# SSD decays: running sums broadcast by DMA into SBUF, differences on VectorE

## The chip, the cores and the metric

The kernel runs on one core of a Trainium2 chip. The metric is the time of one execution on the device in microseconds, as the median of a few runs. A core has TensorE (PE: matmuls from SBUF into PSUM; its weight loads, PEld, overlap them), VectorE (DVE), ScalarE (ACT), GpSimd (POOL) and SyncE (SP), which here only issues DMAs. Each engine works through its own list of instructions in order and waits on semaphores for the others.

## The reference, cut to what matters

One decoder layer over 16 meta tokens and 1024 tokens, width 1024, in fp32: an RMSNorm and an input projection, then side by side a stick-breaking attention (8 heads), a Mamba-2 SSD mixer (16 heads of 64 channels, 2 groups, state 128) and a latent attention (MLA, 8 heads); an output projection; a SwiGLU MLP. The change touches the SSD mixer:

```python
dA = dt * a                                   # per token and head
Acs = cumsum(dA, axis=2)                      # running sum within a block of 128 tokens
seg = Acs[:, :, :, None] - Acs[:, :, None, :]
Ldec = exp(where(tri, seg, -inf))             # 128 x 128 decays per block and head
CB = einsum('bclgn,bcsgn->bclsg', Cc, Bc)
y_diag = einsum(..., CB[..., None] * Ldec, X)
decay = exp(Acs[:, :, -1:] - Acs)
states = einsum(..., Bc, X * decay[..., None])
chunk_decay = exp(Acs[:, :, -1])              # carry * chunk_decay + states, over the blocks
y_off = einsum(..., Cc, prev) * exp(Acs)[..., None]
```

## The kernel before, in words

All sequences are held feature-major (features over the partitions, tokens along the row), and the tokens fall into nine blocks: one of 16 meta tokens and eight of 128. Each large projection is done as three fp32r matmuls of a high and a low half (lines 144 to 146 for most, 908 to 910 for V). The program is written as units of work (projections, convolutions, attention rows, SSD chunks, latent projections). A scheduler lays them out: it runs through a simulated timeline and fixes the order of the instructions on each engine from priorities, dependences and the buffers that are free; while one unit waits, matmuls of others are put on TensorE ("fillers"). So an edit in one unit moves the instructions of its neighbours.

`running_sums` (line 461) is called early. One matmul with a triangle gives the running sums as `AT` (tokens over the partitions, 9 blocks x 16 heads). Each of three chunks of tokens is transposed to `acs` (16 heads over the partitions, tokens along the row), copied by ScalarE, and split on VectorE into three bf16 parts, rows 0, 32 and 64 of `A3` (lines 476 to 482).

`ssd_chunk(c)` (line 756) is called for the nine blocks, and in each for two groups g of eight heads. By name:
- `y` = xs times d_skip (GpSimd, line 765); `X` = transposed x times the step size (VectorE, 774).
- `R`: the running sum of four heads, equal over all 128 partitions. It is made by a matmul of the 0/1 matrix `sel` with `A3` for each head (line 794), into a pool of two PSUM tiles, `rps`.
- `cd`, `dec`: the block's decay and its decay to the block's end (796, 797, 811); `ea` = exp(R) (803); `L` = exp of minus the rectified difference AT - R (ScalarE: `Relu` per head, 806, then one `Exp`, 816).
- `Xd` = X times dec (GpSimd, 812); `cbm` = the product of the group's B and C under the triangle (818, 820); `L` times `cbm` (821).
- `yo`, `sps`, `yd`: the matmuls from the carried state (825), into the state (829), and within the block (841), in a pool of two PSUM tiles, `yps`. `ea` times `yo` (826), the state `S` times `cd` on GpSimd (833) and plus `sps` (836), `y` plus `ea` on GpSimd (846), `y` plus `yd` (847).
- `y` is stored by ScalarE's DMA queue; `xs` and `bc` (B and C) are loaded by SP's (761, 762).

Other names: `wlo` (133) is the low half of a weight, made on GpSimd; `grow` (518) sums squares of the SSD output on GpSimd; `Q` (614) is an eviction of the stick-breaking attention; `d_ps` is the PSUM tile of a projection; line 173 holds the transposes that spread a row of norms over the partitions; line 328 and `ptg` belong to the stick-breaking attention.

Of the kernel before, what the change touches and what calls it, by code (L numbers as in the profile page):

```python
# [11 lines left out]
F32 = mybir.dt.float32  # L12
F32R = mybir.dt.float32r
BF16 = mybir.dt.bfloat16
AF = mybir.ActivationFunctionType
ALU = mybir.AluOpType
AX = mybir.AxisListType
PSUM = bass.MemoryType.PSUM
# [5 lines left out]
META = 16  # L24
T = SEQ + META
# [34 lines left out]
def tile_hybrid_block(ctx: ExitStack, tc: tile.TileContext, a: dict):  # L60
    nc = tc.nc
    act, dve, pool, pe, sp = nc.scalar, nc.vector, nc.gpsimd, nc.tensor, nc.sync
# [10 lines left out]
    dram = ctx.enter_context(tc.tile_pool(name="dram", bufs=1, space=DRAM))  # L73
# [22 lines left out]
    s_qn = dram.tile([4, 128, SEQ], F32, name="s_qn")  # L96
    s_qr = dram.tile([2, 128, SEQ], F32, name="s_qr")
    s_v = dram.tile([9, 128, 512], F32, name="s_v")
    s_inv = dram.tile([MLA_HEADS, SEQ], F32, name="s_inv")


# [84 lines left out]
    keep = hn_stack.enter_context(tc.tile_pool(name="keep", bufs=1))  # L186
    AT = keep.tile([128, 9, 16], F32, name="AT")
    DT = keep.tile([128, 9, 16], F32, name="DT")
    A3 = keep.tile([80, T], BF16, name="A3")
    tri = keep.tile([128, 128], F32, name="tri")  # L190
    fl = hn_stack.enter_context(tc.tile_pool(name="fl", bufs=2))

# [268 lines left out]
    def running_sums(d1):  # L461
        NC = 9 * 16
        pt = tp.tile([128, 512], F32, tag="tp", name="acum")
        pe.matmul(pt[:, :NC], tri, d1, start=True, stop=True)
        dve.tensor_copy(AT.rearrange("p b h -> p (b h)"), pt[:, :NC])

        pool.memset(A3, 0.0)
        for i, (t0, n) in enumerate(CH_ALL):
            acs = fill_tile("craw" if i == 2 else "cacc", "acs")[:16]
            pt = tp.tile([128, 512], F32, tag="tp", name="acst")  # L470
            for b in range(3 * i, 3 * i + 3):
                b0, w = BLOCKS[b]
                pe.transpose(pt[:16, b0 - t0 : b0 - t0 + w], AT[:w, b, :], ident[:w, :w])
            c = slice(t0, t0 + n)
            act.copy(acs[:, :n], pt[:16, :n])
            dve.tensor_copy(A3[0:16, c], acs[:, :n])
            dve.tensor_tensor(acs[:, :n], acs[:, :n], A3[0:16, c], op=ALU.subtract)
            dve.tensor_copy(A3[32:48, c], acs[:, :n])
            a2 = fl.tile([16, 384], BF16, tag="csig", name="a2")
            dve.tensor_copy(a2[:, :n], acs[:, :n])  # L480
            dve.tensor_tensor(acs[:, :n], acs[:, :n], a2[:, :n], op=ALU.subtract)
            dve.tensor_copy(A3[64:80, c], acs[:, :n])

    def conv_unit(u):

# [163 lines left out]
    for i, (q0, qn) in enumerate(((0, 256), (256, 384), (640, 384))):  # L649
        c0, n = CH_ALL[i]  # L650
        if i < 2:
# [9 lines left out]
            r, row = stats[i]  # L661
# [80 lines left out]
    with ExitStack() as st:  # L742
        la = st.enter_context(tc.tile_pool(name="la", bufs=1, side="right", reuse_waits="tile"))
        p2_st = ExitStack()
        p2 = p2_st.enter_context(tc.tile_pool(name="p2", bufs=2, side="right", reuse_waits="tile"))
        rps = st.enter_context(tc.tile_pool(name="rps", bufs=2, space=PSUM, reuse_waits="tile"))
        yps = st.enter_context(tc.tile_pool(name="yps", bufs=2, space=PSUM, reuse_waits="tile"))
        seli = p2.tile([80, 16], F32, bufs=1, name="seli")
        sp.dma_start(seli, a["sel"])
        sel = p2.tile([80, 16, 128], BF16, bufs=1, name="sel")  # L750
        dve.tensor_copy(sel, seli.unsqueeze(2).to_broadcast([80, 16, 128]))
        dsk = p2.tile([128, 8], F32, bufs=1, name="dsk")
        sp.dma_start(dsk, a["d_skip"])
        S = [p2.tile([128, 512], F32, bufs=1, name=f"S{g}") for g in range(2)]
# [1 line left out]
        def ssd_chunk(c):  # L756
            n = META if c == 0 else 128
            t0 = 0 if c == 0 else META + 128 * (c - 1)
# [9 lines left out]
            for g in range(2):  # L768
                gs = slice(512 * g, 512 * (g + 1))
                hs = slice(8 * g, 8 * g + 8)  # L770
# [12 lines left out]
            for g in range(2):  # L783
                gs = slice(512 * g, 512 * (g + 1))
                hs = slice(8 * g, 8 * g + 8)
                cd = p2.tile([128, 8], F32, tag="cd", name="cd")
                dec = p2.tile([128, 8], F32, tag="dec", name="dec")
                L = p2.tile([128, 8, 128], F32, tag="L", name="L")
                ea = p2.tile([128, 4, 128], F32, tag="yt", bufs=1, name="ea")
                for q in range(2):  # L790
                    R = rps.tile([128, 4, 128], F32, tag="R", name="R")
                    qs = slice(4 * q, 4 * q + 4)
                    for h in range(4):
                        pe.matmul(R[:, h, :n], sel[:, 8 * g + 4 * q + h, :], A3[:, t0 : t0 + n], start=True, stop=True)
                    if c < 8:
                        act.activation(cd[:, qs], R[:, :, n - 1], AF.Exp)
                        dve.tensor_tensor(
                            dec[:n, qs], R[:n, :, n - 1], AT[:n, c, 8 * g + 4 * q : 8 * g + 4 * q + 4], op=ALU.subtract
                        )
                    if c > 0:  # L800
                        for e in range(2):
                            half = slice(64 * e, 64 * e + 64)
                            act.activation(ea[half, 2 * q : 2 * q + 2], R[half, e::2, :], AF.Exp)
                        for h in range(4):
                            hh = 4 * q + h
                            act.activation(
                                L[:, hh, :], R[:, h, :], AF.Relu, scale=-1.0,
                                bias=AT[:, c, 8 * g + hh : 8 * g + hh + 1],
                            )
                if c < 8:  # L810
                    act.activation(dec[:n], dec[:n], AF.Exp)
                    pool.tensor_tensor(
                        heads(Xd[:n, gs]), heads(X[:n, gs]), dec[:n].unsqueeze(2).to_broadcast([n, 8, 64]), op=ALU.mult
                    )
                if c > 0:
                    act.activation(L, L, AF.Exp, scale=-1.0)
                    pcb = tp.tile([128, 512], F32, tag="tp", name="cbp")
                    pe.matmul(pcb[:, :128], bc[:, g, :], bc[:, 2 + g, :], start=True, stop=True)
                    cbm = p2.tile([128, 128], F32, tag="cbm", name="cbm")
                    dve.tensor_tensor(cbm, pcb[:, :128], tri, op=ALU.mult)  # L820
                    dve.tensor_tensor(L, L, cbm.unsqueeze(1).to_broadcast([128, 8, 128]), op=ALU.mult)
                    yo = yps.tile([128, 512], F32, tag="y", name="yo")
                    for j in range(4):
                        ts = slice(128 * j, 128 * (j + 1))
                        pe.matmul(yo[:, ts], S[g][:, ts], bc[:, 2 + g, :], start=True, stop=True)
                    dve.tensor_tensor(ea, ea, yo.rearrange("p (j t) -> p j t", j=4), op=ALU.mult)
                if c < 8:
                    sps = yps.tile([128, 512], F32, tag="y", name="sps")
                    pe.matmul(sps, btok[:n, g * 128 : (g + 1) * 128], Xd[:n, gs], start=True, stop=True)
                    if c == 0:  # L830
                        dve.tensor_copy(S[g], sps)
                    else:
                        pool.tensor_tensor(
                            heads(S[g]), heads(S[g]), cd.unsqueeze(2).to_broadcast([128, 8, 64]), op=ALU.mult
                        )
                        dve.tensor_tensor(S[g], S[g], sps, op=ALU.add)
                if c > 0:
                    yd = yps.tile([128, 512], F32, tag="y", name="yd")
                    for h in range(8):
                        hh = 8 * g + h  # L840
                        pe.matmul(
                            yd[64 * (h % 2) : 64 * (h % 2) + 64, 128 * (h // 2) : 128 * (h // 2 + 1)],
                            X[:, hh * 64 : (hh + 1) * 64], L[:, h, :], start=True, stop=True,
                        )
                    yg = y[:, 4 * g : 4 * g + 4]
                    pool.tensor_tensor(yg, yg, ea, op=ALU.add)
                    dve.tensor_tensor(yg, yg, yd.rearrange("p (j t) -> p j t", j=4), op=ALU.add)
# [55 lines left out]
        for b, (t0, w) in enumerate(BLOCKS):  # L903
# [7 lines left out]
            t = row_tile("vtok")  # L911
# [18 lines left out]
        for c0, n in CH_SHORT:  # L930
            c = slice(c0, c0 + n)
# [767 lines left out]
def _layout(x, meta_tokens, mix_norm_g, w_in, conv_w, conv_b, dt_bias, a_log, d_skip, ssm_norm_g,  # L1699
# [16 lines left out]
    inv = (np.float32(10000.0) ** (-np.arange(0, 32, 2, dtype=np.float32) / np.float32(32))).astype(np.float32)  # L1716
    ang = (pos[:, None] * inv[None, :]).astype(np.float32)
    cos, sin = np.cos(ang).T.astype(np.float32), np.sin(ang).T.astype(np.float32)
    sel = np.zeros((80, 16), np.float32)
    for r in (0, 32, 64):  # L1720
        sel[r : r + 16] = np.eye(16)
    return {
        "xT": xn.T.reshape(KT, 128, T),
        "gmix": _cols(mix_norm_g[0]),
# [25 lines left out]
        "k_tab": np.concatenate([cos, cos, -sin, sin], axis=0),  # L1750
        "q_cos": np.tile(cos[:, META:], (8, 1)),
        "q_sin": np.tile(sin[:, META:], (8, 1)),
        "sel": sel,
    }


# [18 lines left out]
```

## Time and profile before

| | us |
|---|---|
| median of 3 runs | 1745.81 (1743.37 to 1752.36) |
| the profiled execution | 1744.0, its span 1742.3 |
| mean granted TensorE clock | 0.989 of full speed |
| busy: PE / DVE / ACT / POOL | 1688.7 (97%) / 1140.2 (65%) / 846.0 (49%) / 717.3 (41%) |
| running sums: instructions of `running_sums` on VectorE | 121.5 to 134.0 from the span's start |
| SSD stage | about 470 to 613 |

Times in the profile are microseconds from the span's start unless they are marked ns. A line of a group names the code line, engine, operation, output and input tile with their shapes, the count, the busy time and the mean ns of one, then the idle time of the engine ahead of it and what ended it. A line of the timeline has the start, the duration, the engine and line, and in brackets how long the engine had been idle and which instruction released it. The profile's time excludes what lies around the span; the runs' times include it (1744.0 against 1742.3).

### The profile page before, as it was taken

To read this page: it belongs to the slowest core of one execution; us is meant where nothing else is said; L and a number is where in the kernel's file an instruction comes from. 1 tells how busy PE (TensorE), PEld (TensorE's weight loads), DVE (VectorE), ACT (ScalarE), POOL (GpSimd) and SP (SyncE) were. 2 spreads that over 40 slices of the span, in tenths; PEclk is the share of its full clock that TensorE was granted. 3 is DMA by queue.
4 is the path that set the end of the run, shared out by engine and by line. 5 is a ranking of instruction groups with operands and counts; after the bars stand their busy time and mean duration, and the time that the engine had idled before them with its cause. 6 is when DMAs were issued, how large, how long until landed. Compare 5 with 4: busy or idle time off the path is not lost.

```text
span 1742.3 us, 26429 instructions
## 1 busy us (share of the span) xinstructions
PE 1688.7 (97%) x9673; PEld 1479.6 (85%) x9673; DVE 1140.2 (65%) x1773; ACT 846.0 (49%) x1811; POOL 717.3 (41%) x514
## 2 busy tenths in 40 slices
PE   8889999999999999999999999999999999999998
PEld 7879989999987888998888878788888888878887
DVE  7777676678455644556576556966666656688644
ACT  6555565656477727776455425432223222343333
POOL 3233335344567537553331445635555555200012
PEclk9999999999999999999999999999999999999999
DMA  4321232122534465348222452232322233999602
GB/s 164 72 67 62 69 89 80 59 69 78 154 115 121 149 219 167 107 130 282 68 78 65 103 180 73 70 99 92 114 91 97 96 104 106 328 398 358 235 1 98
DMA packets 145639, 222.35 MB, mean 128 GB/s; under 512 B 24722, under 2 KB 84148, under 8 KB 145508
## 3 DMA queue, kind: packets, MB, share of 16 engines
q1 hardware_dynamic: 126112, 205.09, 36.6%
q10 hardware_dynamic: 19396, 15.56, 2.9%
q8 instruction: 76, 1.25, 0.3%
q14 instruction: 55, 0.45, 0.1%
HBM read 157.56 MB, written 63.04 MB: 127 GB/s over the span
## 4 chain that ended last, share of the span: by engine, by line
PE 80%; DVE 6%; DMA 6%; ACT 3%; issue 2%; POOL 2%; SPq 0%; ACTq 0%; DVEq 0%; POOLq 0%
PE d_ps L144 9%; PE d_ps L146 9%; PE d_ps L145 9%; PE b_ps L1283 8%; PE b_ps L1282 8%; PE b_ps L1281 8%; PE b_ps L1566 2%; PE b_ps L1567 2%; PE b_ps L1565 2%; PE ptg L326 2%; PE ptg L328 1%; PE pv L305 1%; PE pv L304 1%; DMA raw<-s_osbl 1%; PE sc_ps L991 1%
## 5 line engine op out<-in xcount | busy, mean ns | idle before, releaser
L144 PE MATMUL d_ps<-hnh,whi 128*128 128x384 f32 (+6 forms) x744 | 247.4, 333 | 7.8 <-DVE KS L607 5.4
L146 PE MATMUL d_ps<-hnl,whi 128*128 128x384 f32 (+6 forms) x744 | 248.4, 334 | 0.0
L145 PE MATMUL d_ps<-hnh,wlo 128*128 128x384 f32 (+6 forms) x744 | 246.7, 332 | 0.1
L133 POOL TENSOR_TENSOR wlo<-wraw,whi 128x1024 fp32r<-128x1024 f32 (+1 forms) x57 | 136.8, 2401 | 218.2 <-ACT whi L131 194.1
L144 PEld LDWEIGHTS d_ps<-hnh,whi 128*128 128x128 f32 (+1 forms) x744 | 141.0, 190 | 12.7 <-issue 6.0
L146 PEld LDWEIGHTS d_ps<-hnl,whi 128*128 128x128 f32 (+1 forms) x744 | 140.8, 189 | 3.1 <-issue 0.7
L145 PEld LDWEIGHTS d_ps<-hnh,wlo 128*128 128x128 f32 (+1 forms) x744 | 140.9, 189 | 2.8 <-POOL wlo L133 0.4
L1282 PE MATMUL b_ps<-T,wl 128*128 128x512 f32 x352 | 139.6, 397 | 1.3 <-POOL wl L1113 1.3
L1283 PE MATMUL b_ps<-T,wh 128*128 128x512 f32 x352 | 139.2, 397 | 1.3 <-DVE T L1113 1.3
L1281 PE MATMUL b_ps<-T,wh 128*128 128x512 f32 x352 | 139.3, 397 | 0.0
L312 DVE TENSOR_TENSOR pl<-ptg,ph 128x512 fp32r<-128x512 f32 (+1 forms) x160 | 99.8, 628 | 55.3 <-ACT ph L311 54.1
L1112 ACT CAST op<-raw 128x1024 fp32r<-128x1024 f32 x69 | 71.2, 1050 | 111.3 <-PE d_ps L1567 55.1
L311 ACT CAST ph<-ptg 128x512 fp32r<-128x512 f32 (+1 forms) x160 | 85.6, 542 | 52.3 <-PE ptg L328 32.8
L1113 DVE TENSOR_TENSOR op<-raw,op 128x1024 fp32r<-128x1024 f32 x69 | 84.9, 1240 | 39.5 <-ACT op L1112 39.4
L696 DVE TENSOR_TENSOR_SCAN cm<-cm,sb_mask 128x144 f32<-128x144 f32 (+3 forms) x64 | 97.1, 1523 | 7.4 <-ACT cm L694 6.8
L1113 POOL TENSOR_TENSOR wlo<-raw,whi 128x1024 fp32r<-128x1024 f32 x18 | 45.4, 2521 | 110.3 <-ACT whi L1112 110.3
L1113 POOL TENSOR_TENSOR wl<-raw,wh 128x512 fp32r<-128x512 f32 x46 | 74.9, 1635 | 30.5 <-ACT wh L1112 30.3
L1112 ACT CAST wh<-raw 128x512 fp32r<-128x512 f32 x88 | 53.2, 616 | 69.5 <-PE b_ps L1283 69.4
L131 ACT CAST whi<-wraw 128x1024 fp32r<-128x1024 f32 (+1 forms) x57 | 58.9, 1033 | 55.4 <-PE d_ps L146 30.6
L1119 POOL TENSOR_TENSOR tt<-tt 128x512 f32<-128x512 f32 (+1 forms) x8 | 8.1, 1015 | 188.4 <-ACT tt L1637 188.2
L1282 PEld LDWEIGHTS b_ps<-T,wl 128*128 128x128 f32 x352 | 66.8, 190 | 17.4 <-POOL wl L1113 1.6
L1116 DVE TENSOR_TENSOR raw<-raw 128x512 f32<-128x512 f32 x58 | 53.2, 925 | 43.3 <-DMA raw<-in_w_gate_dram 38.4
(440 smaller groups left out, 5120.0 us busy)
## 6 DMA issues: line engine op xcount, KB each, us to landing
raw<-in_w_down_dram SPq DMA_DIRECT2D x99, 256.0 KB, 5.3
s_hops<-gs SPq DMA_DIRECT2D x63, 256.0 KB, 2.0
raw<-s_hops SPq DMA_DIRECT2D x63, 256.0 KB, 5.4
raw<-in_w_gate_dram SPq DMA_DIRECT2D x22, 512.0 KB, 3.6
raw<-in_w_up_dram SPq DMA_DIRECT2D x22, 512.0 KB, 4.2
wraw<-in_w_o_dram SPq DMA_DIRECT2D x16, 512.0 KB, 3.8
wraw<-in_w_xbc_dram SPq DMA_DIRECT2D x12, 512.0 KB, 4.2
s_xs<-csig SPq DMA_DIRECT2D x24, 192.0 KB, 2.6
```

The source lines that it names most:

```text
L133: pool.tensor_tensor(lo[:, :cols], raw[:, :cols], f32(hi[:, :cols]), op=ALU.subtract)
L144: pe.matmul(ps[:m, :n], wh, mh, start=(kt == 0), stop=False)
L145: pe.matmul(ps[:m, :n], wl, mh, start=False, stop=False)
L146: pe.matmul(ps[:m, :n], wh, ml, start=False, stop=(kt == nkt - 1))
L311: act.copy(ph[:, :n], pt[:, :n])
L312: dve.tensor_tensor(pl[:, :n], pt[:, :n], f32(ph[:, :n]), op=ALU.subtract)
L696: dve.tensor_tensor_scan(rev, rev, sb_mask[:, T - n_all :][:, ::-1], 1.0, ALU.mult, ALU.max)
L1112: act.copy(hi, value)
L1113: eng.tensor_tensor(lo, value, f32(hi), op=ALU.subtract)
L1281: pe.matmul(banks[j], hi[:, ks], UH[u][k], start=start and k == 0, stop=False, skip_group_check=skip)
L1282: pe.matmul(banks[j], lo[:, ks], UH[u][k], start=False, stop=False, skip_group_check=skip)
L1283: pe.matmul(banks[j], hi[:, ks], UL[u][k], start=False, stop=stop and k == 3, skip_group_check=skip)
```

## The change

The running sums are no longer split into bf16 parts. Each `acs` goes to a scratch array in DRAM, `s_sum` (9 blocks x 16 heads x 128 tokens), by SP's DMA queue. `ssd_chunk` then loads one tile `R` of 8 heads x 128 tokens per group from there, the same row into all 128 partitions, into SBUF with four buffers. The `sel` input, `A3`, the R matmuls and the PSUM pool `rps` are gone, and `yps` has four buffers instead of two. `cd`, `dec` and `ea` are computed for eight heads at once. `L` is made by VectorE: per head one `tensor_scalar` takes R minus the head's column of `AT`, and the smaller of that and 0; ScalarE's `Exp` then has scale 1 in place of -1. In the code after, most lines of this part carry other numbers: R's load is 782, `dec` 785, `ea` 789, the new operation 791, `Xd` 796, `L` exp 800, `L` times `cbm` 805, `yo` 809, `sps` 813, `S` 820, `yd` 825, `y` 830 and 831.

```diff
     s_v = dram.tile([9, 128, 512], F32, name="s_v")
+    s_sum = dram.tile([9, 16, 128], F32, name="s_sum")
...
     DT = keep.tile([128, 9, 16], F32, name="DT")
-    A3 = keep.tile([80, T], BF16, name="A3")
...
 
-        pool.memset(A3, 0.0)
         for i, (t0, n) in enumerate(CH_ALL):
             acs = fill_tile("craw" if i == 2 else "cacc", "acs")[:16]
             pt = tp.tile([128, 512], F32, tag="tp", name="acst")
             for b in range(3 * i, 3 * i + 3):
                 b0, w = BLOCKS[b]
                 pe.transpose(pt[:16, b0 - t0 : b0 - t0 + w], AT[:w, b, :], ident[:w, :w])
-            c = slice(t0, t0 + n)
             act.copy(acs[:, :n], pt[:16, :n])
-            dve.tensor_copy(A3[0:16, c], acs[:, :n])
-            dve.tensor_tensor(acs[:, :n], acs[:, :n], A3[0:16, c], op=ALU.subtract)
-            dve.tensor_copy(A3[32:48, c], acs[:, :n])
-            a2 = fl.tile([16, 384], BF16, tag="csig", name="a2")
-            dve.tensor_copy(a2[:, :n], acs[:, :n])
-            dve.tensor_tensor(acs[:, :n], acs[:, :n], a2[:, :n], op=ALU.subtract)
-            dve.tensor_copy(A3[64:80, c], acs[:, :n])
+            if i == 0:
+                sp.dma_start(s_sum[0, :, :META], acs[:, :META])
+            nb = min(3, n // 128)
+            src = acs[:, n - 128 * nb : n].rearrange("h (b t) -> h b t", b=nb)
+            sp.dma_start(s_sum[3 * i + 3 - nb : 3 * i + 3].rearrange("b h t -> h b t"), src)
...
         p2 = p2_st.enter_context(tc.tile_pool(name="p2", bufs=2, side="right", reuse_waits="tile"))
-        rps = st.enter_context(tc.tile_pool(name="rps", bufs=2, space=PSUM, reuse_waits="tile"))
-        yps = st.enter_context(tc.tile_pool(name="yps", bufs=2, space=PSUM, reuse_waits="tile"))
-        seli = p2.tile([80, 16], F32, bufs=1, name="seli")
-        sp.dma_start(seli, a["sel"])
-        sel = p2.tile([80, 16, 128], BF16, bufs=1, name="sel")
-        dve.tensor_copy(sel, seli.unsqueeze(2).to_broadcast([80, 16, 128]))
+        yps = st.enter_context(tc.tile_pool(name="yps", bufs=4, space=PSUM, reuse_waits="tile"))
...
                 ea = p2.tile([128, 4, 128], F32, tag="yt", bufs=1, name="ea")
-                for q in range(2):
-                    R = rps.tile([128, 4, 128], F32, tag="R", name="R")
-                    qs = slice(4 * q, 4 * q + 4)
-                    for h in range(4):
-                        pe.matmul(R[:, h, :n], sel[:, 8 * g + 4 * q + h, :], A3[:, t0 : t0 + n], start=True, stop=True)
-                    if c < 8:
-                        act.activation(cd[:, qs], R[:, :, n - 1], AF.Exp)
-                        dve.tensor_tensor(
-                            dec[:n, qs], R[:n, :, n - 1], AT[:n, c, 8 * g + 4 * q : 8 * g + 4 * q + 4], op=ALU.subtract
+                R = p2.tile([128, 8, 128], F32, tag="R", bufs=4, name="R")
+                sp.dma_start(R[:, :, :n], s_sum[c, hs, :n].partition_broadcast(128))
+                if c < 8:
+                    act.activation(cd, R[:, :, n - 1], AF.Exp)
+                    dve.tensor_tensor(dec[:n], R[:n, :, n - 1], AT[:n, c, hs], op=ALU.subtract)
+                if c > 0:
+                    for e in range(2):
+                        half = slice(64 * e, 64 * e + 64)
+                        act.activation(ea[half], R[half, e::2, :], AF.Exp)
+                    for h in range(8):
+                        dve.tensor_scalar(
+                            L[:, h, :], R[:, h, :], AT[:, c, 8 * g + h : 8 * g + h + 1], 0.0, op0=ALU.subtract, op1=ALU.min
                         )
-                    if c > 0:
-                        for e in range(2):
-                            half = slice(64 * e, 64 * e + 64)
-                            act.activation(ea[half, 2 * q : 2 * q + 2], R[half, e::2, :], AF.Exp)
-                        for h in range(4):
-                            hh = 4 * q + h
-                            act.activation(
-                                L[:, hh, :], R[:, h, :], AF.Relu, scale=-1.0,
-                                bias=AT[:, c, 8 * g + hh : 8 * g + hh + 1],
-                            )
                 if c < 8:
                     act.activation(dec[:n], dec[:n], AF.Exp)
                     pool.tensor_tensor(
                         heads(Xd[:n, gs]), heads(X[:n, gs]), dec[:n].unsqueeze(2).to_broadcast([n, 8, 64]), op=ALU.mult
                     )
                 if c > 0:
-                    act.activation(L, L, AF.Exp, scale=-1.0)
+                    act.activation(L, L, AF.Exp)
```

The scheduler lays the work out anew up to the end of the SSD stage; from the latent units after it TensorE's order is the same. Three places follow. The first is VectorE at the running sums; `Q` is an eviction of the stick-breaking attention. Before:

```order
L614 TENSOR_TENSOR Q<-d_ps,Q 64x512
L481 TENSOR_TENSOR acs<-acs,a_1085 16x272
L478 CAST A_119<-acs 16x384
L480 CAST a_1098<-acs 16x384
L482 CAST A_119<-acs 16x272
L614 TENSOR_TENSOR Q<-d_ps,Q 64x512
```

After:

```order
L465 COPY AT<-acum 128x144
L610 TENSOR_TENSOR Q<-d_ps,Q 64x512 x4
L319 TENSOR_TENSOR pm<-ptm,pm 16x256
L495 SCALAR_TENSOR_TENSOR cacc<-d_ps,cw,cacc 128x269
L495 SCALAR_TENSOR_TENSOR cacc<-d_ps,cw,cacc 128x270
```

The Q evictions stood between the casts and subtractions of the split; now they follow one another.

The second is VectorE in the middle of the SSD stage. Before:

```order
L820 TENSOR_TENSOR cbm<-cbp,tri 128x128
L847 TENSOR_TENSOR y<-y,yd 128x512
L826 TENSOR_TENSOR ea<-ea,yo 128x512
L821 TENSOR_TENSOR L<-L,cbm 128x1024
L797 TENSOR_TENSOR dec<-R,AT 128x4 x2
L820 TENSOR_TENSOR cbm<-cbp,tri 128x128
L836 TENSOR_TENSOR S_5436<-S_5436,sps 128x512
L847 TENSOR_TENSOR y<-y,yd 128x512
L774 TENSOR_TENSOR X<-xtp,DT 128x512
L826 TENSOR_TENSOR ea<-ea,yo 128x512
L821 TENSOR_TENSOR L<-L,cbm 128x1024
```

After:

```order
L831 TENSOR_TENSOR y<-y,yd 128x512
L791 TENSOR_SCALAR L<-R,AT 128x128 x8
L810 TENSOR_TENSOR ea<-ea,yo 128x512
L820 TENSOR_TENSOR S_5411<-S_5411,sps 128x512
L791 TENSOR_SCALAR L<-R,AT 128x128 x7
L765 TENSOR_TENSOR X<-xtp,DT 128x512
L791 TENSOR_SCALAR L<-R,AT 128x128
L785 TENSOR_TENSOR dec<-R,AT 128x8
L831 TENSOR_TENSOR y<-y,yd 128x512
L810 TENSOR_TENSOR ea<-ea,yo 128x512
```

The new operations of a group stand together, ahead of evictions (`ea`, `S`, `X`) for which TensorE and GpSimd wait.

The third is TensorE at the end of the SSD stage; `d_ps<-lhi` are the latent projections, `d_ps<-whi` those of V. Before:

```order
L144 MATMUL d_ps<-lhi,whi 128x384
L145 MATMUL d_ps<-lhi,wlo 128x384
L146 MATMUL d_ps<-llo,whi 128x384
L173 MATMUL d_ps<-identr,rc 128x128 x4
L841 MATMUL yd<-L,X 64x128 x8
L173 MATMUL d_ps<-identr,rc 128x128 x4
L144 MATMUL d_ps<-lhi,whi 128x512
L145 MATMUL d_ps<-lhi,wlo 128x512
```

After:

```order
L892 MATMUL d_ps<-whi,lhi 128x512
L893 MATMUL d_ps<-whi,llo 128x512
L825 MATMUL yd<-L,X 64x128 x8
L894 MATMUL d_ps<-wlo,lhi 128x512
L892 MATMUL d_ps<-whi,lhi 128x512
L893 MATMUL d_ps<-whi,llo 128x512
L894 MATMUL d_ps<-wlo,lhi 128x512
```

Behind the last `yd` now stand 19 matmuls of V, and after those 72 latent matmuls (24 of 272 columns, 48 of 384) and eight transposes of line 173, ahead of the first latent matmul of 512 columns; before, four transposes alone stood there.

More of the change, by code (lines that the diff above doesn't have):

```diff
@@ L1718, in _layout @@
     cos, sin = np.cos(ang).T.astype(np.float32), np.sin(ang).T.astype(np.float32)
-    sel = np.zeros((80, 16), np.float32)
-    for r in (0, 32, 64):
-        sel[r : r + 16] = np.eye(16)
     return {
@@ L1752, in _layout @@
         "q_sin": np.tile(sin[:, META:], (8, 1)),
-        "sel": sel,
     }
```

## The prediction

> **What bounds the kernel now.** I read first the chain that ended last, by engine, then the busy time of each engine in the stretches that the change touches (columns: stretch, its length, then busy us and instructions of PE, PEld, DVE, ACT and POOL, the granted clock of PE, the DMA share and GB/s).
>
> ```profile
> PE 80%; DVE 6%; DMA 6%; ACT 3%; issue 2%; POOL 2%; SPq 0%; ACTq 0%; DVEq 0%; POOLq 0%
> 100.00:120.00 20.00, 16.56 (x71) 13.49 (x70) 16.55 (x27) 7.62 (x15) 6.84 (x5) 0.91 0.16 48
> 480.00:613.00 133.00, 129.02 (x1004) 107.40 (x1002) 79.03 (x139) 100.69 (x296) 87.03 (x64) 1.00 0.43 133
> ```
>
> The SSD stage is the second stretch. TensorE works 129.0 of 133 us there, so TensorE sets its pace; ScalarE has 32 us to spare, VectorE 54, GpSimd 46. The first stretch stands at the running sums, where VectorE is the busy one and TensorE waits.
>
> How long a chunk takes is read from the last matmuls of each group, `yd` (line 841), and from what TensorE does around the end of the stage.
>
> ```profile
> L841 PE MATMUL yd<-L,X x256: 272/273/324, 491.0 to 611.6; 128*64 128x128 f32 x128
> 610.73 1.09 PE L841 MATMUL yd<-L,X 128*64 128x128 f32 x16 [0.32 <-DVE L L821]
> 611.75 1.16 PE L173 MATMUL d_ps<-identr,rc 128*128 128x128 f32 x8
> 613.19 0.51 PE L144 MATMUL d_ps<-lhi,whi 128*128 128x512 f32 x1 [0.28 <-ACT lhi L873]
> ```
>
> Sixteen groups (two per chunk, eight chunks) begin between 491.0 and 610.73: 7.5 chunks in 119.7 us, 16.0 us per chunk, with filler matmuls of other units between them. At 613.19 the next stage begins; from there on TensorE's order is the same in both kernels, so the change is decided by when the work ahead of that row is done.
>
> **Part 1, the R matmuls leave TensorE.**
>
> ```profile
> 477.88 0.61 PE L794 MATMUL R<-A,sel 80*128 80x128 bf16 x8
> 478.33 0.78 PE L155 MATMUL d_ps<-ones,grow 128*128 128x1 f32 x6
> 505.10 0.39 PE L794 MATMUL R<-A,sel 80*128 80x128 bf16 x4
> 505.30 0.42 PE L144 MATMUL d_ps<-hnh,whi 128*128 128x384 f32 x1
> 505.56 0.34 PE L145 MATMUL d_ps<-hnh,wlo 128*128 128x384 f32 x1
> 505.73 0.33 PE L146 MATMUL d_ps<-hnl,whi 128*128 128x384 f32 x1
> ```
>
> Eight of them take 478.33 − 477.88 = 0.45 us, 0.056 each; 144 make 8.1. The fp32r matmul that follows such a group holds TensorE 505.56 − 505.30 = 0.26 us instead of 0.17; 0.09 for each of about 28 groups makes 2.5. TensorE is spared 10.6 us, all of it on the path while TensorE sets the pace.
>
> **Part 2, the bf16 parts leave VectorE at the running sums.**
>
> ```profile
> 124.38 2.02 DVE L481 TENSOR_TENSOR acs<-acs,a 16x272 f32<-16x272 f32 x1
> 127.50 0.69 DVE L614 TENSOR_TENSOR Q<-d_ps,Q 64x512 fp32r<-64x512 f32 x1
> 128.25 0.44 PE L144 MATMUL d_ps<-hnh,whi 128*128 128x388 f32 x1 [2.08 <-DVE Q L614]
> ```
>
> A projection matmul waits 2.08 us for a Q eviction that stood behind the subtraction of 2.02 us and the casts. All 18 such operations go, and with them this wait: −2.1 us. The other TensorE waits of that stretch come from work that stays; I give them nothing. Four small stores on SP's queue take the operations' place; their reader comes some 340 us later.
>
> **Part 3, ScalarE is relieved, VectorE is loaded.** The operations concerned, by line, in the SSD stage (busy us, mean ns, then idle time ahead):
>
> ```profile
> L806 ACT ACTIVATE L<-R,AT 128x128 f32<-128x128 f32 x128 | 36.8, 370 | 0.6
> L821 DVE TENSOR_TENSOR L<-L,cbm 128x1024 f32<-128x1024 f32 x16 | 25.9, 1618 | 23.8 <-ACT L L816 23.8
> L774 DVE TENSOR_TENSOR X<-xtp,DT 128x512 f32<-128x512 f32 (+1 forms) x18 | 12.3, 682 | 1.0 <-PE xtp L773 0.7
> L847 DVE TENSOR_TENSOR y<-y,yd 128x512 f32<-128x512 f32 x16 | 11.0, 686 | 10.8 <-PE yd L841 6.9 <-issue 1.7 <-POOL y L846 1.2
> L826 DVE TENSOR_TENSOR ea<-ea,yo 128x512 f32<-128x512 f32 x16 | 11.0, 685 | 9.8 <-ACT ea L803 3.9 <-PE yo L825 2.9 <-PE xtp L773 1.8
> L836 DVE TENSOR_TENSOR S<-S,sps 128x512 f32<-128x512 f32 x14 | 9.5, 679 | 3.6 <-PE sps L829 3.0 <-POOL S L833 0.5
> L820 DVE TENSOR_TENSOR cbm<-cbp,tri 128x128 f32<-128x128 f32 x16 | 4.5, 282 | 1.8 <-PE cbp L818 1.8
> L765 POOL TENSOR_TENSOR y<-xs,dsk 128x1024 f32<-128x1024 f32 x8 | 15.2, 1897 | 14.1 <-DMA s_y<-y 14.1
> L133 POOL TENSOR_TENSOR wlo<-wraw,whi 128x1024 fp32r<-128x1024 f32 (+1 forms) x6 | 13.1, 2188 | 4.0 <-ACT whi L131 4.0
> L518 POOL TENSOR_TENSOR grow<-grow,sq 128x384 f32<-128x384 f32 (+1 forms) x7 | 6.5, 927 | 1.4 <-ACT sq L517 1.4
> ```
>
> ScalarE loses the 128 rectified copies of line 806; as it does not set the pace, that is worth nothing by itself. The same holds for `cd`, `dec` and `ea` on eight heads at once. Four `yps` buffers in place of two can at most save TensorE's waits in the stage, 133 − 129 = 4.0 us; those now come from VectorE (0.32 in the `yd` row above), so I count nothing. VectorE gets 128 subtract-and-clamp operations of 128x128 from SBUF to SBUF, 16 per chunk. What one of them costs depends on GpSimd, as the next rows show:
>
> ```profile
> L450 DVE TENSOR_SCALAR DT<-d x1: 235/235/235, 101.1 to 101.1; 128x144 f32<-128x144 f32 x1
> L454 DVE TENSOR_SCALAR DT<-DT x1: 2227/2227/2227, 111.3 to 111.3; 128x144 f32<-128x144 f32 x1
> 525.42 0.69 DVE L826 TENSOR_TENSOR ea<-ea,yo 128x512 f32<-128x512 f32 x1 [0.39 <-PE yo L825]
> 526.02 0.28 DVE L820 TENSOR_TENSOR cbm<-cbp,tri 128x128 f32<-128x128 f32 x1
> 526.25 1.05 POOL L812 TENSOR_TENSOR Xd<-X,dec 128x512 f32<-128x512 f32 x1 [1.90 <-ACT dec L811]
> 527.26 1.05 POOL L833 TENSOR_TENSOR S<-S,cd 128x512 f32<-128x512 f32 x1
> 528.26 2.38 POOL L133 TENSOR_TENSOR wlo<-wraw,whi 128x1024 fp32r<-128x1024 f32 x1
> 528.41 3.30 DVE L821 TENSOR_TENSOR L<-L,cbm 128x1024 f32<-128x1024 f32 x1 [2.11 <-ACT L L816]
> 530.59 2.27 POOL L846 TENSOR_TENSOR y<-y,ea 128x512 f32<-128x512 f32 x1
> 497.78 1.29 POOL L846 TENSOR_TENSOR y<-y,ea 128x512 f32<-128x512 f32 x1 [2.04 <-DVE dec L797]
> ```
>
> A TENSOR_SCALAR of one shape lasts 235 ns at one place and 2,227 at another. The multiplication of line 821, whose two inputs lie in SBUF, lasts 1.2 us when free; begun at 528.41, it lasts 3.30: GpSimd's `wlo` holds until 530.64, and then it runs its own length. GpSimd's next `y` lasts 2.27 for its 1.29, until that one is done. So SBUF work of the two engines goes one after the other. Evictions with one input in PSUM (525.42, 526.02) keep their length.
>
> One new operation: successors on VectorE start about 0.08 us before an operation's end (525.42 + 0.69 against 526.02 gives 0.09), so 235 ns at 144 columns become a spacing of 0.15, of which I let 0.10 block GpSimd.
>
> Per chunk, VectorE's own work is then two each of lines 774, 847, 826, 836, 820 (6.0, less 0.8 for the overlap: 5.2), two multiplications of 1.15 (2.3), 16 × 0.15 = 2.4 and 0.1 for `dec`: 10.0 us. GpSimd's is 1.9 (line 765), 2 × 1.05 (`Xd`), 2 × 1.05 (`S`) and 2 × 1.29 (`y`), 8.7, and of lines 133 and 518 (19.6 us in 8.3 chunks, 2.4, part of it waiting) 2.0: 10.6.
>
> If the pair is never idle, a chunk takes GpSimd's 10.6 + 2.2 (multiplications) + 1.6 (new operations) = 14.4 us. If the two engines never overlap at all, it takes 10.0 + 10.6 = 20.6. Between them I walked through one steady chunk in the changed order: VectorE's 10.0 us plus its waits behind GpSimd (rest of `y` 0.7, `S` 1.0, `Xd` 1.0, `y` 0.8, `S` 1.0, `Xd` 1.0, `y` 1.1, filler at least 0.2: 6.8, less 0.5 in which it would have waited for TensorE anyway) make **16.3 us**. It lies nearer the lower end because half of VectorE's work reads PSUM.
>
> TensorE's own work per chunk falls: the 117 us of the 119.7 above, less 25 groups' share of 10.6 (9.4), less the fillers that go behind (15.9, next part), leave 91.7 in 7.5 chunks: 12.2. TensorE then waits 4 us per chunk, and VectorE with GpSimd sets the pace.
>
> [...]
>
> **Part 4, the fillers.** The scheduler places less filler work under the SSD chain: behind the last `yd` now stand 19 matmuls of V, 24 latent ones of 272 columns and 48 of 384, which ran ahead of it before.
>
> ```profile
> 562.14 0.40 PE L909 MATMUL d_ps<-whi,llo 128*128 128x512 f32 x1
> 562.37 0.40 PE L910 MATMUL d_ps<-wlo,lhi 128*128 128x512 f32 x1
> ```
>
> At 0.235 (these two rows), 0.175 (505.56 to 505.73, for 384) and that times 272/384 = 0.125: 4.5 + 3.0 + 8.4 = 15.9 us, and 1.4 for the transposes of line 173 that stand there today (611.75 to 613.19).
>
> **Part 5, the loads.** Eighteen 512 KB loads of R join SP's queue.
>
> ```profile
> grow<-s_inv SPq DMA_DIRECT2D x6, 256.0 KB, 4.5
> xs<-s_xs SPq DMA_DIRECT2D x8, 512.0 KB, 4.3
> ```
>
> A repeated row of 256 KB lands in 4.5 us, a plain 512 KB in 4.3. Four buffers are two chunks' worth, so each load is issued about a chunk (16 us) before its use, at a DMA share of 0.43 for the stage. I cost them at nothing; if each came 4.5 late once per chunk it would be up to +30, if only the first does, +4.5.
>
> **The sum.** First `yd` as before at 491.0; six chunks of 16.3 (97.8); the lighter last chunk (no `S`, `Xd`) 13.5; its second group 8 × 0.15 + 1.2 + 1.1 = 3.5; the fillers 15.9 + 1.4: 623.1, against 613.2. That is +9.9; with −2.1 from part 2, +7.8. The profiled execution was 1744.0, so 1751.8; the median of the runs lies 1.8 above it: 1753.6, said as **1754 us**. The break-even pace is 16.3 − 7.8/7 = 15.2 us per chunk.
>
> **The rivals.**
> 1. *TensorE stays the bound, not slower.* The new operations fit into gaps and the pair does not limit; decided by a pace below 15.2. Gain 10.6 + 2.1 = 12.7: 1733; with the pair at its lower bound of 14.4, 1745.8 + 7.8 − 7 × 1.9 = 1740. For it: VectorE's 54 idle us, and that the scalar of the new operation is a column of `AT`, a form whose blocking no row here shows. Against: line 454.
> [...]
> 2. *The two engines hardly overlap.* Each of the 16 operations waits behind a GpSimd instruction, a pace of 18.5 to 20.6: 7 × 2.2 to 7 × 4.3 on top, 1769 to 1784. For it: 3.30 and 2.27 above. Against: GpSimd is idle a third of the stage.
> 3. *R comes late.* SP's queue or the DMA engines hold the first loads: 1754 + 4.5 to 9, 1758 to 1763.
> 4. *A slower clock.* Waits of TensorE cost clock: 0.91 in the first stretch above, where waits of 2 us stand. On 12.2 us per chunk that makes 13.4, still under 16.3, so it moves nothing alone.
>
> **How the numbers follow.** My forecast, a pace of 15.4 to 17.5 (1748 to 1763), 0.50; rival 1, 0.24; rival 2, 0.14; rival 3, 0.08; a different reshuffle of the early part, either way, 0.04. Leaving out 0.1 at each end gives 1732 to 1771; the forecast's own range is 1748 to 1763. About 0.5% (8.7 us: 1737 to 1754.5) is what a measurement of this kernel tells from no change: rival 1's better part is faster, 0.19; its worse part and half of the forecast the same, 0.36; the rest slower, 0.45.
>
> **What would show it.** Right: `yd` groups 16 us apart, TensorE's busy share in the stage at 85% or less, the new operations with a mean well above 0.235 us and some above 1 us, lines 821 and 846 longer, and 15 us of fillers behind the last `yd`. Wrong: new operations at 0.2 us throughout, TensorE above 95%, or VectorE waiting for R's DMA.

## The result, and the profile after

The changed kernel takes 1775.1 us (median of 4 runs, 1771.9 to 1780.6) against 1746.1 before: 1.7% slower, ratio 1.0166 with a 95% interval of 1.0142 to 1.0189. The forecast was 1754 us with a range up to 1771. The direction of the slip was seen; its size was 29 us in place of 8. The profiled execution is the slowest of the four, 1780.6 us.

First the chain by engine and the stretches of the changed kernel, with the columns of the prediction's first fence.

```profile
PE 74%; DVE 13%; DMA 6%; issue 3%; ACT 2%; POOL 1%; SPq 1%; DVEq 0%; ACTq 0%; POOLq 0%
100.00:120.00 20.00, 16.53 (x71) 13.32 (x69) 16.25 (x26) 7.32 (x15) 6.55 (x5) 0.91 0.16 48
480.00:641.00 161.00, 134.90 (x901) 109.56 (x899) 135.15 (x254) 66.31 (x123) 97.50 (x67) 0.92 0.54 169
480.00:490.00 10.00, 4.84 (x20) 3.28 (x19) 7.39 (x22) 4.72 (x10) 6.28 (x5) 0.67 1.06 386
490.00:500.00 10.00, 10.00 (x53) 8.89 (x52) 4.85 (x8) 2.33 (x5) 4.84 (x4) 0.82 0.24 68
```

VectorE's share of the chain went from 6% to 13%. The SSD stage is now 161 us long instead of 133. TensorE works 135 of it (84%; before, 97%), VectorE as much. The last two rows show something that the prediction did not have: 5 us of TensorE idle and a granted clock of 0.67, then 0.82, where the stage starts.

The frame of the stage on TensorE: `yd` (line 825 now), the last group, and the first latent matmul of 512 columns.

```profile
L825 PE MATMUL yd<-L,X x256: 272/273/476, 501.4 to 620.4; 128*64 128x128 f32 x128
619.61 1.09 PE L825 MATMUL yd<-L,X 128*64 128x128 f32 x16
637.41 1.97 PE L174 MATMUL d_ps<-identr,rc 128*128 128x128 f32 x16
641.27 0.50 PE L145 MATMUL d_ps<-lhi,whi 128*128 128x512 f32 x1 [1.90 <-ACT lhi L857]
```

The next stage starts 641.27 − 613.19 = 28.1 us later than before, nearly the whole difference of the medians (29.0). Of it, 10.4 is the first `yd` (501.4 against 491.0); from the first group's start to the last group's, the sixteen take about as long as before (118.2 against 119.7 us); and 21.7 us instead of 2.5 lie between the start of the last group and the next stage. This one execution loses 8.5 us more after 641. The other three are 4 to 9 us shorter in all; where, is not on record, and the 8.5 are left out below.

The new operations and their neighbours, by group:

```profile
L791 DVE TENSOR_SCALAR L<-R,AT x128: 267/274/1614, 481.1 to 611.2; 128x128 f32<-128x128 f32 x128
L791 DVE TENSOR_SCALAR L<-R,AT 128x128 f32<-128x128 f32 x128 | 45.4, 420 | 4.0 <-DMA R<-s_sum 4.0
L805 DVE TENSOR_TENSOR L<-L,cbm 128x1024 f32<-128x1024 f32 x16 | 30.8, 1928 | 0.7
L800 ACT ACTIVATE L<-L 128x1024 f32<-128x1024 f32 x16 | 16.9, 1059 | 22.9 <-DVE L L791 22.9
L830 POOL TENSOR_TENSOR y<-y,ea 128x512 f32<-128x512 f32 x16 | 21.5, 1342 | 24.3 <-DVE ea L810 21.6 <-DVE dec L785 2.7
```

Half of the new operations last 0.27 us, the longest 1.61; the multiplication by `cbm` rose from a mean of 1.62 us to 1.93. ScalarE's `Exp` waits 22.9 us for the new operations, GpSimd's `y` 21.6 us for `ea`, which stands behind them on VectorE. That it is GpSimd that holds the long ones up is seen where they end:

```profile
539.47 1.04 POOL L796 TENSOR_TENSOR Xd<-X,dec 128x512 f32<-128x512 f32 x1
539.73 0.86 DVE L791 TENSOR_SCALAR L<-R,AT 128x128 f32<-128x128 f32 x1
```

`Xd` ends at 540.51, and the new operation 0.08 us later. In the same way, each of the 26 new operations that last over 0.4 us ends 0.08 to 0.09 us after an instruction of GpSimd does.

And the start of the stage, where the R of the first full chunk is awaited (timeline of VectorE, ScalarE and TensorE):

```profile
481.07 5.35 DVE L791 TENSOR_SCALAR L<-R,AT 128x128 f32<-128x128 f32 x16 [3.96 <-DMA R<-s_sum]
481.07 0.22 ACT L784 ACTIVATE cd<-R 128x8 f32<-128x8 f32 x1 [4.09 <-DMA R<-s_sum]
484.90 1.06 ACT L800 ACTIVATE L<-L 128x1024 f32<-128x1024 f32 x1 [1.89 <-DVE L L791]
485.86 0.34 ACT L773 COPY btok<-btp 16x256 f32<-16x256 f32 x1
486.35 2.04 PE L813 MATMUL sps<-Xd,btok 16*128 16x512 f32 x2 [5.16 <-ACT btok L773]
489.55 0.52 PE L146 MATMUL d_ps<-hnh,wlo 128*128 128x384 f32 x1
489.87 0.52 PE L147 MATMUL d_ps<-hnl,whi 128*128 128x384 f32 x1
496.04 0.69 DVE L815 COPY S<-sps 128x512 f32<-128x512 f32 x1 [5.03 <-PE sps L813]
```

ScalarE and VectorE stand 4 us before R lands at 481. Behind `cd` on ScalarE stand `ea`, the `Exp` (which waits for the 16 new operations) and then the small copy `btok`; TensorE waits 5.16 us for that copy. Its next matmuls then follow at 0.32 us (489.55 to 489.87) where 384 columns took 0.17 before, at a clock of 0.67; the second `sps` stands behind them, and VectorE waits 5.03 us for it.

### The profile page after: what moved, and what is told of

The parts are those of the page before. It is cut to its first block, busy times and chain, and to the rows that moved or that the text cites. A ratio compares the mean times of both kernels' runs of the same rounds, so it can differ in the third digit from the quotient of the medians.

```text
span 1778.9 us, 26111 instructions
## 1 busy us (share of the span) xinstructions
PE 1698.2 (95%) x9529; PEld 1482.6 (83%) x9529; DVE 1195.6 (67%) x1866; ACT 811.7 (46%) x1635; POOL 721.6 (41%) x513
## 4 chain that ended last, share of the span: by engine, by line
PE 74%; DVE 13%; DMA 6%; issue 3%; ACT 2%; POOL 1%; SPq 1%; DVEq 0%; ACTq 0%; POOLq 0%
PE d_ps L145 8%; PE d_ps L146 8%; PE d_ps L147 8%; PE b_ps L1266 7%; PE b_ps L1267 7%; PE b_ps L1265 7%; PE b_ps L1550 2%; PE b_ps L1551 2%; PE b_ps L1549 2%; DVE L L791 2%; PE ptg L326 2%; PE pv L305 1%; PE ptg L328 1%; DVE cm L692 1%; PE pv L304 1%
## 5 line engine op out<-in xcount | busy, mean ns | idle before, releaser
L692 DVE TENSOR_TENSOR_SCAN cm<-cm,sb_mask 128x144 f32<-128x144 f32 (+3 forms) x64 | 106.3, 1669 | 13.3 <-ACT cm L690 12.8
L1100 DVE TENSOR_TENSOR raw<-raw 128x512 f32<-128x512 f32 x58 | 57.5, 998 | 41.4 <-DMA raw<-in_w_gate_dram 37.7
L145 PE MATMUL d_ps<-raw,whi 128*128 128x512 f32 x192 | 77.8, 405 | 3.7 <-DVE hT L1075 3.7
```

What stands on the lines that cost most here:

```text
L145: pe.matmul(ps[:m, :n], wh, mh, start=(kt == 0), stop=False)
L692: dve.tensor_tensor_scan(rev, rev, sb_mask[:, T - n_all :][:, ::-1], 1.0, ALU.mult, ALU.max)
```

## The experiments

Theory A: the new operations and GpSimd hold each other up, so VectorE sets the pace of a chunk. Theory B: the loss is the late first R, TensorE's wait and the slow clock after it. The order of the work (fillers behind the last `yd`) was the third suspect, and e9 and e11 came to it.

**e1: the differences back on ScalarE, R still loaded.**

```diff
-    dve.tensor_scalar(L[:, h, :], R[:, h, :], AT[...], 0.0, op0=ALU.subtract, op1=ALU.min)
+    act.activation(L[:, h, :], R[:, h, :], AF.Relu, scale=-1.0, bias=AT[...])
...
-    act.activation(L, L, AF.Exp)
+    act.activation(L, L, AF.Exp, scale=-1.0)
```

> The changed kernel, but the rectified differences are made by ScalarE again (Relu per head, from the loaded R in SBUF); the loads of R stay. Theory A (the new VectorE operations and their waits behind GpSimd set the pace of a chunk, 17 us): VectorE loses 16 operations of 0.20 to 1.6 us per chunk, the pace falls below 15.5, and the time falls by 12 to 18 us, from 1775 to 1757-1763. Theory B (the late first load of R, the wait of 5.2 us on TensorE and the half clock after it are the loss): these stay, and the time stays within 5 us of 1775.

Measured: 1747.4 us, ratio to before 1.0012 (0.9998 to 1.0027). All 28 us come back, more than either theory said.

```profile
L825 PE MATMUL yd<-L,X x256: 272/273/476, 496.7 to 594.6; 128*64 128x128 f32 x128
614.75 0.50 PE L145 MATMUL d_ps<-lhi,whi 128*128 128x512 f32 x1 [2.23 <-ACT lhi L857]
480.00:490.00 10.00, 7.82 (x37) 7.25 (x37) 2.96 (x6) 9.46 (x28) 6.68 (x5) 0.83 1.07 379
```

The groups now take 97 us, 13 per chunk, and the start is milder too. `btok` comes as late as in the changed kernel (485.82 against 485.86), as `Relu` operations stand ahead of it; but `X` no longer stands behind VectorE's 16 new operations (481.97 against 486.43), and in this order transposes and fillers stand ahead of `sps`, so TensorE is idle 2.2 us there instead of 5.2. Some 21 us of work are still behind the last `yd`. So VectorE's new work was the loss, but not in the steady pace alone, and the 10.6 us that TensorE is spared do not appear.

**e2: R of the first full chunk loaded early.**

```diff
+    R1 = [keep.tile([128, 8, 128], F32, name="R1") for _ in range(2)]
...
+        for g in range(2):
+            sp.dma_start(R1[g], s_sum[1, 8 * g : 8 * g + 8].partition_broadcast(128))
...
-                R = p2.tile([128, 8, 128], F32, tag="R", bufs=4, name="R")
-                sp.dma_start(R[:, :, :n], s_sum[c, hs, :n].partition_broadcast(128))
+                if c == 1:
+                    R = R1[g]
+                else:
+                    R = p2.tile([128, 8, 128], F32, tag="R", bufs=3, name="R")
+                    sp.dma_start(R[:, :, :n], s_sum[c, hs, :n].partition_broadcast(128))
```

> The changed kernel, but the two R tiles of the first full chunk have buffers of their own and are loaded right after the running sums, some 340 us earlier; three buffers for the others. Theory A: the first yd stands earlier, but the pace stays 17 us; the time falls by at most the 10 us by which the first yd was late, to 1765. Theory B: the wait of 5.2 us and the slow clock from 486 to 494 us go, and nearly all of the 29 us come back, 1750 or less. If the start only shifts the work (fillers ran meanwhile), 1775 stays.

Measured: 1765.6 us, ratio 1.0112 (1.0093 to 1.0132): 9.5 us come back, theory A's figure.

```profile
L832 PE MATMUL yd<-L,X x256: 272/273/476, 492.5 to 618.0; 128*64 128x128 f32 x128
479.42 1.12 PE L820 MATMUL sps<-Xd,btok 16*128 16x512 f32 x2
480.00:490.00 10.00, 10.00 (x60) 8.21 (x59) 4.49 (x10) 2.82 (x7) 6.99 (x6) 1.00 1.00 333
```

The wait of 5.16 us and the low clock are gone together, and the first `yd` stands at 492.5. Theory B is right for about a third of the loss; how much of that is the wait and how much the clock, this run does not tell.

**e3: the differences written into PSUM.** R still comes from SBUF.

```diff
+    Dq = rps.tile([128, 4, 128], F32, tag="Dq", name="Dq")      # one for each half of the group
-    dve.tensor_scalar(L[:, h, :], R[:, h, :], ...)
+    dve.tensor_scalar(Dq[:, h, :], R[:, hh, :], ...)
+    act.activation(L[:, 4 * q : 4 * q + 4], Dq, AF.Exp)
-    yps ... bufs=4
+    rps ... bufs=2, yps ... bufs=2
```

> The changed kernel, but the new VectorE operations write their differences into PSUM (two tiles of four heads) and ScalarE's Exp reads them there and writes L into SBUF; R still comes from SBUF, and the pool of yo, sps, yd has two buffers again. Theory A with the shared SBUF path (operations with source and destination in SBUF wait for GpSimd): none of the new operations lasts above 0.4 us, GpSimd is not held, the pace falls to 14.5-15.5 us, and the time falls by 12 to 20 us, to 1755-1763. If it is the mere number of VectorE operations: pace and time stay as they are, 1770-1780. Theory B: 1775.

Measured: 1738.9 us, ratio 0.9961 (0.9946 to 0.9977): 36 us less than the changed kernel, and less than before. The new operations, of e3 and of e9 (the control, below), as minimum/median/maximum in ns:

```profile
L795 DVE TENSOR_SCALAR Dq<-R,AT x128: 331/346/356, 479.2 to 599.7; 128x128 f32<-128x128 f32 x128
```
```profile
L791 DVE TENSOR_SCALAR L<-R,AT x128: 273/278/2427, 479.0 to 615.7; 128x128 f32<-128x128 f32 x128
```

With the destination in PSUM each is slower when free (346 against 278) and not one of the 128 is held up, although GpSimd is busy 92.91 of the 127 us from 480 to 607. So it is the SBUF-to-SBUF form that waits for GpSimd here (up to 2,427 ns in e9), not the number of operations.

**e9: the control.** e3 also had two `yps` buffers and `Exp` in two halves; here these stay, and the differences go to SBUF again.

> Control for e3_diff_into_PSUM: the changed kernel with what else e3 changed (two buffers of yo, sps, yd, Exp in two halves), but the differences stay in SBUF. Theory A with the shared SBUF path: as the changed kernel, 1768-1780, with single new operations above 1 us. If the buffers or the halves made e3 fast: near 1740.

Measured: 1756.0 us, ratio 1.0054 (1.0033 to 1.0075), between the two answers. e3's 36 us are about 17 for the destination and 19 for the rest; each share contains what the scheduler's new order brings with it.

```profile
L826 PE MATMUL yd<-L,X x256: 272/273/474, 498.6 to 623.2; 128*64 128x128 f32 x128
623.40 0.50 PE L145 MATMUL d_ps<-lhi,whi 128*128 128x512 f32 x1
```

The sixteen groups take longer than in the changed kernel (623.2 against 620.4 for the last matmul), yet the next stage begins 0.2 us after the last `yd` and not 20 later: the fillers lie under the chain again.

**e11: one part of the change undone, two `yps` buffers.**

```diff
-        yps = st.enter_context(tc.tile_pool(name="yps", bufs=4, space=PSUM, reuse_waits="tile"))
+        yps = st.enter_context(tc.tile_pool(name="yps", bufs=2, space=PSUM, reuse_waits="tile"))
```

> The changed kernel with one part undone: two yps buffers in place of four. In its order all V and latent fillers stand ahead of the last yd again. If that placing, and not Exp in halves, made e9 19 us faster than the changed kernel: as e9, 1753-1759, with a pace of 16 to 18 us and 1 to 4 us from the last yd to the next stage. If Exp in halves did it: 1768-1780.

Measured: 1761.3 us, ratio 1.0092 (1.0072 to 1.0113), 14 under the changed kernel and 5 above e9, just outside the range expected for the placing alone. Those 5 us go with the `Exp` in halves, the one difference between this run and e9.

```profile
625.49 1.09 PE L825 MATMUL yd<-L,X 128*64 128x128 f32 x16
629.29 0.50 PE L145 MATMUL d_ps<-lhi,whi 128*128 128x512 f32 x1 [1.62 <-ACT lrow L731]
```

So four `yps` buffers, which were to relieve TensorE, let the scheduler finish the SSD chain with fewer fillers beside it. A likely reason is that the chain was faster on its simulated timeline than on the chip; the simulated times are not on record. On the chip VectorE held the chain up, TensorE was busy 84% of the stage, and the fillers came afterwards. Undoing it costs chain time (124 us of groups for 118) and is still a gain.

**e4: the differences on VectorE, read from R in PSUM, in the kernel before.** Its edit puts `dve.tensor_scalar` in the place of the `Relu` of line 806 and gives `Exp` the scale 1; the matmuls stay.

> The kernel before, but the rectified differences are made by VectorE, read from R in PSUM; the R matmuls, the bf16 parts and the order of the loads are those of before. Theory A with the shared SBUF path: reads from PSUM do not wait for GpSimd, so the 16 operations add about 3 us per chunk to VectorE's 79 of 133 us and stay hidden: 1744-1750. If the number of VectorE operations matters: slower by 10 us or more. Theory B: no load of R, so nothing is lost: 1744-1750.

Measured: 1748.2 us, ratio 1.0017 (1.0001 to 1.0034). The same 128 operations on VectorE cost 3 us (0.2 to 6) when their source is in PSUM, and none is held up:

```profile
L806 DVE TENSOR_SCALAR L<-R,AT x128: 339/344/353, 486.1 to 615.7; 128x128 f32<-128x128 f32 x128
```

**e6: y = xs times d_skip on ScalarE,** which takes 1.9 us per chunk from GpSimd.

> The changed kernel with y = xs times d_skip made by ScalarE (eight operations of 128x128) and no longer by GpSimd (1.9 us per chunk). Theory A with the shared SBUF path: the new operations meet less GpSimd work, the pace falls from 17 by 0.5 to 1.9 us per chunk, and the time falls by 4 to 13 us, to 1762-1771. If GpSimd does not hold VectorE: 1775.

Measured: 1763.9 us, ratio 1.0100 (1.0074 to 1.0126), 11 under the changed kernel.

```profile
L806 DVE TENSOR_TENSOR L<-L,cbm 128x1024 f32<-128x1024 f32 x16 | 26.6, 1669 | 0.5
```

```profile
L792 DVE TENSOR_SCALAR L<-R,AT 128x128 f32<-128x128 f32 x128 | 45.4, 420 | 4.2 <-DMA R<-s_sum 4.2
```

The multiplication falls from 1.93 to 1.67 us, 4 us in all, but the new operations keep their mean of 420 ns. The time came out as theory A expected; that the new operations meet less GpSimd work was not seen, and where the other 7 us come from was not settled.

**e7: one bf16 part instead of three, in the kernel before,** the prediction's part 2 alone.

> The kernel before, but only the first of the three bf16 parts of the running sums is made (rows 32 to 47 and 64 to 79 of A3 stay zero), so that 15 of 18 VectorE operations leave the running sums; the SSD stage is as before. By the prediction's part 2 the wait of 2.1 us goes and the time falls by 2 us, to 1743-1744. Rival: the gain is given back before the SSD stage by other waits in the new order, as in the changed kernel, where waits of 1.2, 1.1 and 2.2 us stand at 177, 283 and 429 us: within 1 us of the kernel before.

Measured: 1746.8 us, ratio 1.0007 (0.9993 to 1.0021): the rival. The wait at 128 us is gone, and TensorE is full there, but a new one stands further on:

```profile
120.00:140.00 20.00, 20.00 (x135) 18.85 (x134) 13.78 (x20) 11.18 (x24) 5.93 (x4) 1.00 0.11 34
432.67 0.59 PE L144 MATMUL d_ps<-hnh,whi 128*128 128x388 f32 x1 [2.12 <-DVE cacc L493]
```

**e5, e8, e10, e12: towards a faster kernel.** e5 is e3 with the early R of e2; e8 adds e6's edit to that; e10 is e3 with `Exp` writing back into PSUM and the multiplication by `cbm` reading there; e12 is e1 with two `yps` buffers.

> Differences into PSUM as in e3_diff_into_PSUM, and the early load of the first R as in e2_early_R. If the two losses are separate, the start gains some 3 us more (there the first yd stands at 496.1, with the early load at 492.5): 1733-1737, 9 to 13 us under the kernel before. If fillers cover the late start anyway: 1738-1740.

> As e5_psum_and_early_R, and y = xs times d_skip on ScalarE. If waits of the chain behind GpSimd still cost: 2 to 8 us under e5. If TensorE paces by then: the same as e5 within 2 us.

> As e3_diff_into_PSUM, but Exp leaves the decays in PSUM too, and the multiplication by cbm reads them there in two halves, so that it has one input in SBUF in place of two. Theory A with the shared SBUF path: the multiplications lose their waits behind GpSimd (1.2 us for 1024 columns when free, up to 2.9 in the changed kernel), each half lasts below 0.8 us, and the time is 3 to 10 us under e3's 1739. If the two PSUM tiles, now held until the multiplication, delay the next differences: 1739-1750.

> As e1_relu_on_scalar (differences on ScalarE, R loaded), with two yps buffers: in its order all V fillers and half of the latent ones stand ahead of the last yd. e1 had a pace of 13 us with TensorE not full, and 21 us of work behind the last yd. If the fillers are what e1 lost, 5 to 12 us come back: 1735-1742. If two buffers slow the chain by as much: 1745-1750.

Measured, with the ratio to before: e5 1741.8 (0.9977, 0.9962 to 0.9991); e8 1742.6 (0.9977, 0.9963 to 0.9991); e10 1738.5 (0.9948, 0.9927 to 0.9969); e12 1742.3 (0.9981, 0.9968 to 0.9993). The early R, worth 9.5 us in e2, adds nothing to e3, nor does e6's edit: the first `yd` stands at 496.5 in e5 and at 496.1 in e3, so the late R does not set it there. e5 lies a little above both ranges expected for it. e12 brings back 5 us of e1's time, the low end of what was expected if the fillers were its loss. In e10 the multiplication is never held up (minimum/median/maximum 674/682/696 ns):

```profile
L813 DVE TENSOR_TENSOR L<-Dq,cbm 128x512 f32<-128x512 f32 x32 | 21.4, 683 | 0.3
```

but its time stands beside e3's within their intervals, not 3 to 10 us under it. All four and e3 are faster than the kernel before, e3 and e10 most, by 0.4 to 0.5%. The gains do not add up: the 9.5, 14 and 17 us of e2, e11 and the destination were each measured with something else still in the way.

## Why the prediction was wrong in size

By its own steps:

- **Part 1, TensorE spared 10.6 us: not seen in the changed kernel,** where TensorE did not set the pace. No median came to the 1733 us of the forecast's first rival; e10, the best, is 7 us under before. In e10's profiled execution the next stage begins 9.4 us earlier than before (603.79 against 613.19), so most of the gain can appear once VectorE is not held up; that execution then loses it behind this row, with the same number of matmuls, and why was not settled.

```profile
603.79 0.50 PE L145 MATMUL d_ps<-lhi,whi 128*128 128x512 f32 x1
```

- **Part 2, −2.1: gone, then given back.** e7 shows both. In the changed kernel TensorE waits 2.04 us at 431.5 for `cacc`, as it does in e7 at 432.67. I gave the other waits nothing, as coming from work that stays; the new order made others.
- **Part 3, the waiting for GpSimd: right, and shown (e3 against e9, and the ends of the long operations).** The steady pace was put at 16.3 us and came out at 16.7; the seven chunks took 114.7 us where the sum had 97.8 + 13.5 = 111.3, +3.4. One term that was short is the new operation's spacing: 0.15 taken, 0.196 the median between free neighbours in the changed kernel's trace, 16 × 0.046 = 0.7 us per chunk. Over seven chunks that is more than the 3.4, so some other term was put a little too high; which one is open. The last group took 4.5 (616.16 to 620.63) instead of 3.5: +1.0.
- **The first `yd`, taken unmoved at 491.0: the step that failed.** It came 10.4 us late. Part 5 costed the loads at nothing because each has a chunk's time; the first full chunk's have not, since the four R loads queue with the other loads of the new stage at a DMA share of 0.95 (470 to 480 us) and 1.06 (480 to 490), and land after a median of 7.5 us. VectorE waiting for R's DMA (3.96 us at 481.07) is a sign of being wrong that the prediction itself had named. Rival 3 had this wait with 4.5 to 9 us, and a chance of 8%. What it lacked is the order on the engines: on ScalarE the late R holds `cd` and with it `btok` behind it, and on TensorE `sps` stands next and waits for `btok`. A later first `yd` is no loss by itself, as fillers can run meanwhile (e3 has it at 496.1 and is fast); that it was one here, e2's 9.5 us show.
- **Rival 4, the clock, "moves nothing alone": wrong at this place.** It was reckoned on a steady chunk. At the start the slowed fillers stand ahead of `sps` on TensorE, so by the order the slow clock is on the chain. An estimate from the rows: 13 fillers between 489.55 and 493.70 at 0.32 instead of 0.175 us (granted clock 0.50 from 489.5 to 493.6) make 1.9 us; no run separates it from the wait.
- **Part 4, the fillers behind: right, 20.6 us for 17.3** (+3.3: the fillers take 16.8 for 15.9; the transposes, 1.97, and TensorE's wait of 1.90 for `lhi` make 3.9 for 1.4). e9 and e11 show that this placing was worth about as much as the waiting for GpSimd (14 us in e11, 17 between e9 and e3). The prediction had its price, but not its cause; it gave the `yps` buffers nothing, and they are what moved the fillers (e11).

Together 10.4 + 3.4 + 1.0 + 3.3 = 18.1 us, but for rounding the distance from the 623.1 of the sum to the 641.27 at which the next stage began; with the 2.1 us that part 2 took off and that did not show, the sum missed that row by some 20 us. Rival 2's 1769 to 1784 holds the measured time, but by luck: its pace of 18.5 or more never came, the longest chunk being 17.6 us. Two small slips in the prediction's numbers decide nothing: TensorE's 117 us of the 119.7 are 115.9 by the trace, and paces of 15.4 and 17.5 give 1747 and 1762, not 1748 and 1763.

## What to carry to other kernels

Before work is moved to an engine with idle time, look at what its operands live in: here 128 small operations cost 3 us with their source in PSUM (e4), and about 17 us more from SBUF to SBUF than with their destination in PSUM (e9 against e3). Follow the first pass of a new load by itself, through every engine's queue, since the steady state says nothing about it. Where a simulated timeline sets the order, look at where the filler work ends up: here bringing it back under the chain recovered 14 of the 29 us (e11).

## What the runs showed of the hardware

A wait of TensorE of 2.04 us was followed by a slow clock in the changed kernel:

```profile
431.50 0.41 PE L145 MATMUL d_ps<-hnh,whi 128*128 128x388 f32 x1 [2.04 <-DVE cacc L495]
431.92 0.34 PE L147 MATMUL d_ps<-hnl,whi 128*128 128x388 f32 x1
432.10 0.41 PE L145 MATMUL d_ps<-hnh,whi 128*128 128x388 f32 x1
432.62 0.53 PE L147 MATMUL d_ps<-hnl,whi 128*128 128x388 f32 x1
432.94 0.53 PE L145 MATMUL d_ps<-hnh,whi 128*128 128x388 f32 x1
```

The spacing of 388 columns goes from 0.18 (431.92 to 432.10) to 0.32 us (432.62 to 432.94) within about a microsecond of TensorE's resuming, and the granted clock from 432.3 to 435.2 us is 0.50. It did not happen every time. In the kernel before, a wait of 1.95 us was not followed by it:

```profile
237.93 0.41 PE L144 MATMUL d_ps<-hnh,whi 128*128 128x384 f32 x1 [1.95 <-DVE KS L607]
238.88 0.34 PE L146 MATMUL d_ps<-hnl,whi 128*128 128x384 f32 x1
239.05 0.34 PE L144 MATMUL d_ps<-hnh,whi 128*128 128x384 f32 x1
```

The spacing there stays at 0.17, and the granted clock from 238 to 250 us is 1.00. What else decides it was not tried.

The second is what one of the 128 operations takes with PSUM and without: a median of 346 ns and never more than 356 with a PSUM destination (e3), 344 and at most 353 with a PSUM source (e4), 274 ns and up to 1,614 from SBUF to SBUF (278 and up to 2,427 in e9). What makes the SBUF-to-SBUF form wait for GpSimd no row shows: the "shared SBUF path" of the expectations is the author's name for this waiting.
